# Loading V one pair of units earlier in a single load queue, with a fifth V buffer

## Chip, core and metric

The kernel runs on one core of a Trainium2 chip. The metric is the device time of one execution in microseconds (us). Eight executions of the kernel before gave a median of 132.31 us (131.64 to 133.25).

## What is computed

Q, K and V are float32 of shape (8, 12, 512, 64): 96 heads of 512 rows by 64 columns. The attention is across the 64 columns, not across the rows:

```python
Q_norm = Q / (np.linalg.norm(Q, axis=-2, keepdims=True) + 1e-10)
K_norm = K / (np.linalg.norm(K, axis=-2, keepdims=True) + 1e-10)
attn = np.einsum('bhnd,bhne->bhde', Q_norm, K_norm)
attn = np.exp(attn - np.max(attn, axis=-1, keepdims=True))
attn = attn / (np.sum(attn, axis=-1, keepdims=True) + 1e-10)
return np.einsum('bhnd,bhde->bhne', V, attn).astype(np.float32)
```

## The kernel before, in words

The 96 heads are worked on in 24 units of 4 heads. A unit's Q is 512 KB, its K 512 KB, its result 512 KB. V comes by pairs of units, 1 MB at a time, so there are twelve V loads, V0 to V11; V of pair w serves units 2w and 2w+1. In this document Q7 is the load of Q of unit 7, S7 the store of the result of unit 7.

All loads and stores are issued by SP (SyncE), in one queue, in the order in which the program text reaches `load_qk` (L69), `load_v` (L75) and `store` (L79). SP is in order: an issue that has to wait holds back all behind it. Two things can hold an issue. One is its buffer: Q and K have five buffers each, V four, the results ten, and a load needs the last reader of its buffer to be done (for V that is the cast of the second unit of the pair, four pairs earlier). The other is its completion counter: the queue has eight of them, used in turn, and a transfer takes the counter of the eighth transfer before it, which must have landed. So up to eight transfers are in flight, and where nothing else holds the queue, the time of an issue dates the landing of the eighth transfer before.

The order is written out by hand ("manual schedule"). The main loop (L228) has steps s = 0 to 23. Step s does, among other things:

- on SP: load Q and K of unit s+3 (L230), then as many V loads as L231 asks for, then stores of results that are done (L234). `outs_by(s)` (L62), (s - 3) * 9 // 10, is the number of units whose output is made by the end of step s; n1 in the code.
- on DVE (VectorE), from step 5 on in this order: half of the cast of V of a unit (`cast_v`, L96; only where a V unit is due), the cast of Q of unit s+1 (`cast_q`, L84), the softmax division of unit s-2 (`normalise`, L143 to L147), the norms of unit s from the gram matrix (`norms`, L115), the scaling of the logits of unit s-1 (L135), the cast of K of unit s+1 (`cast_k`, L87).
- on PE (TensorE): the gram matrix of unit s (`grams`, L103, 64 matmuls), the transposes to logits of unit s-1 (L131), the outputs of finished units (`outs`, L188), a copy to the upper partitions (`doubled`, L176), the transposes of V (`vtrans`, L155).
- on ACT (ScalarE): the other half of the V cast (L96), `keep_kq` (L108), the exponentials (L139), the copies of the outputs (L192), L177 and the copy of transposed V (L159). POOL (GpSimd) does the power -1/2 (L120) and scales K (L125).

The V units cast at the end of the loop are 16 and 17 (V8) in steps 20 and 21, and 18 and 19 (V9) in steps 22 and 23. After the loop a tail (L268) makes the outputs of the last six units, 18 to 23; there V is transposed in float32 straight from its load buffer (`vtrans_f32`, L170), so V10 and V11 are read without a cast.

In program order the end of SP's queue before reads, by steps: 18: Q21 K21 V8 S9; 19: Q22 K22 S10; 20: Q23 K23 V9 S11; 21: S12; 22: V10 S13; 23: S14; tail: V11 S15, S16, and so on to S23, whose store is in two halves.

Of the kernel before, what the change touches and what calls it, by code (L numbers as in the profile page):

```python
# [27 lines left out]
def kernel(  # L28
# [10 lines left out]
    U = B * H // HU  # L39
# [6 lines left out]

    const = ctx.enter_context(tc.tile_pool(name="const", bufs=1))
    qp = ctx.enter_context(tc.tile_pool(name="qp", bufs=5))
    vp = ctx.enter_context(tc.tile_pool(name="vp", bufs=4))
    vbp = ctx.enter_context(tc.tile_pool(name="vbp", bufs=3))  # L50
    qkp = ctx.enter_context(tc.tile_pool(name="qkp", bufs=4))
    vtp = ctx.enter_context(tc.tile_pool(name="vtp", bufs=3))
# [9 lines left out]
    def outs_by(s):  # L62

        return max(0, (s - 3) * 9 // 10)
# [10 lines left out]
    def load_v(w):  # L75
        vf[w] = vp.tile([128, 2 * R * D], F32, name="vf")
        nc.sync.dma_start(out=vf[w], in_=Vf[w])

    def store(u, g=slice(0, SV)):  # L79
        nc.sync.dma_start(out=Of[u][:, g], in_=so[u][:, g].rearrange("p s t d -> p s (t d)"))  # L80
# [8 lines left out]
    def cast_v(v):  # L89

        w, i = divmod(v, 2)
        if i == 0:
            vb[w] = vbp.tile([128, A, TP, 2 * D], BF16, name="vb")
        x = vf[w].rearrange("p (a t d) -> p a t d", a=A, d=2 * D)
        for t, copy in ((2 * i, nc.scalar.copy), (2 * i + 1, nc.vector.tensor_copy)):
            copy(vb[w][:, :, t], x[:, :, t])  # L96
# [32 lines left out]
    def logits(u):  # L129
        for h in range(HU):  # L130
            nc.tensor.transpose(lg[:, h, :], kqs[u][D:, h, :], ident[D:, D:])  # L131

    def scale_q(u):
        s = sl[u] = small.tile([D, HU, D], F32, name="sl")
        nc.vector.tensor_tensor(out=s, in0=lg, in1=rq[u][0:D, :, None].to_broadcast([D, HU, D]), op=ALU.mult)  # L135

    def exps(u):
        e = ex[u] = small.tile([D, HU, D], F32, name="ex")
        nc.scalar.activation(e, sl[u], AF.Exp)  # L139

    def normalise(u):
        s = small.tile([D, HU], F32, name="esum")
        nc.vector.reduce_sum(out=s, in_=ex[u], axis=AX.X)  # L143
        ri = small.tile([D, HU], F32, name="rinv")
        nc.vector.reciprocal(ri, s)
        a = abuf[u % len(abuf)]
        nc.vector.tensor_tensor(out=a[0:D, :, 0, :], in0=ex[u], in1=ri[:, :, None].to_broadcast([D, HU, D]), op=ALU.mult)  # L147

    def vtrans(v):

        w, i = divmod(v, 2)
        ps = ps_v.tile([128, A, 2, 128], BF16, name="vps")
        for t in range(2):
            for a in range(A):
                nc.tensor.transpose(ps[:, a, t, :], vb[w][:, a, 2 * i + t, :], identb)  # L155

        if i == 0:
            vt[w] = vtp.tile([128, TP, 128, A], BF16, name="vt")
        nc.scalar.copy(vt[w][:, 2 * i:2 * i + 2], ps.rearrange("p a t c -> p t c a"))  # L159
# [13 lines left out]
    def doubled(u):  # L173

        a = abuf[u % len(abuf)]
        nc.tensor.matmul(dup[D:], identb[0:D, 0:D], a[0:D, :, 0, :], tile_position=(0, D))  # L176
        nc.scalar.copy(a[D:, :, 1, :], dup[D:])  # L177

    def outs(u, copies=(nc.scalar.copy, nc.scalar.copy)):
        s = so[u] = sop.tile([128, SV, TP, 2 * D], F32, name="so")  # L180
        a = abuf[u % len(abuf)]
        v = vt[u // 2][:, :, u % 2 * 64:(u % 2 + 1) * 64]
        for g in range(SV):
            po = ps_o.tile([128, TP, 2 * D], F32, name="po")
            for t in range(TP):
                for x in range(2):
                    h = 2 * g + x
                    nc.tensor.matmul(  # L188
                        po[MV * x:MV * (x + 1), t, :], v[:, t, NP * h:NP * (h + 1), :].rearrange("p c a -> p (c a)"),
                        a[:, h].rearrange("p a d -> p (a d)"), tile_position=(0, MV * x),  # L190
                    )
            copies[g](s[:, g], po)  # L192
# [21 lines left out]
    def clear(i):  # L214

        nc.scalar.copy(abuf[i].rearrange("p h a d -> p (h a d)"), zeros)
# [4 lines left out]
    def on(f, u):  # L221
        if 0 <= u < U:
            f(u)
# [3 lines left out]
    nv, nst, nt = 0, 0, 0  # L227
    for s in range(U):  # L228
        n0, n1 = outs_by(s - 1), outs_by(s)
        on(load_qk, s + LOAD_AHEAD)  # L230
        while nv < (min(U, n1 + 5) // 2 if s >= 3 else 1):  # L231
            load_v(nv)
            nv += 1
        while nst < n1 - 3:  # L234
            store(nst)
            nst += 1
        new = range(nt, max(0, min(s - 2, n1 + 2)))
        if s > 4:
            for v in new:
                cast_v(v)  # L240
        on(cast_q, s + 1)
        on(normalise, s - 2)
        on(grams, s)
        on(norms, s)
        on(keep_kq, s)
        on(scale_k, s)
        on(logits, s - 1)
        on(scale_q, s - 1)
        on(exps, s - 1)
        on(cast_k, s + 1)  # L250
        if s <= 4:
            for v in new:
                cast_v(v)
        for v in range(n0, n1):
            outs(v)
        on(doubled, s - 2)
        if 6 <= s + 5 < len(abuf):
            clear(s + 5)
        for v in new:
            vtrans(v)  # L260
            nt = v + 1
# [4 lines left out]
    both = (nc.scalar.copy, nc.vector.tensor_copy)  # L266

    for i, u in enumerate(range(n1, U)):  # L268
        while nv < min(U, u + 6) // 2:
            load_v(nv)  # L270
            nv += 1
        store(u - 3)
        if i == 0:
            normalise(last - 1)
        if i == 2:
            scale_q(last)
            exps(last)
        if i == 3:
            normalise(last)
        on(vtrans_f32, u + 2)  # L280
        if i == 1:
            doubled(last - 1)
        if i == 3:
            doubled(last)
        outs(u, both)
        if i == 1:
            logits(last)
# [33 lines left out]
```

## Time and profile before

| what | value |
|---|---|
| median of 8 executions | 132.31 us (131.64 to 133.25) |
| the eight, sorted | 131.64, 131.70, 131.82, 131.93, 132.69, 132.97, 132.99, 133.25 |
| the profiled execution, its time | 131.70 us |
| its span, first to last instruction | 129.9 us (1.8 us lie around it) |
| mean granted TensorE clock | 0.913 |
| busy share of the span: DVE, ACT, PE, POOL | 74%, 70%, 65%, 50% |
| HBM read, written | 37.75 MB, 12.58 MB |

All times within the execution are us from the start of the span, on one core. An idle time in brackets behind an instruction is that of its engine just before it, with what ended it. L96 is line 96 of the kernel printed above. "SPq" is SP's queue of DMA issues; PE, DVE and ACT are the engines' names above.

### The profile page before, as it was taken

The numbers are of one execution on the slowest core, as the hardware profiler recorded it, in microseconds if no ns is written. First come the engines' busy times: TensorE is split into PE (matmuls) and PEld (weight loads), VectorE is DVE, ScalarE is ACT, GpSimd is POOL, SyncE is SP. The second block draws the span as 40 slices with busy tenths as digits, with TensorE's granted clock in tenths as the row PEclk, the third lists the DMA queues.
The fourth block names the chain that finished last, engine by engine and source line by source line (L and its number), as shares of the span: only waits on it lengthen the run. The fifth ranks groups of instructions, "written<-read, shape, count | busy, mean of one in ns | idle before, by whom it ended". The sixth has DMA issues, their size and how long they took to land.

```text
span 129.9 us, 5391 instructions
## 1 busy us (share of the span) xinstructions
PE 85.0 (65%) x2232; PEld 65.2 (50%) x2232; DVE 95.5 (74%) x366; ACT 91.2 (70%) x171; POOL 65.4 (50%) x57
## 2 busy tenths in 40 slices
PE   0147673959866766849873798576755797859640
PEld 0136551738644555628652576354543585637420
DVE  0465869596998997996892999779659759657840
ACT  7610353665999999888983569897966885997530
POOL 4014872662688558565762766577706635600000
PEclk9999999999999999996897579999999559999965
DMA  4999999999999999999999999999999999988775
GB/s 135 400 414 431 404 410 414 407 410 420 404 419 402 408 431 394 417 425 405 402 424 404 419 406 429 405 412 429 404 409 419 414 413 414 409 345 326 281 284 205
DMA packets 15208, 50.67 MB, mean 390 GB/s; under 512 B 1360, under 2 KB 1360, under 8 KB 13648
## 3 DMA queue, kind: packets, MB, share of 16 engines
q1 hardware_dynamic: 15184, 50.34, 97.0%
q8 instruction: 17, 0.28, 0.8%
q14 instruction: 7, 0.06, 0.1%
HBM read 37.75 MB, written 12.58 MB: 387 GB/s over the span
## 4 chain that ended last, share of the span: by engine, by line
DMA 50%; ACT 18%; PE 12%; DVE 11%; issue 4%; SPq 0%; ACTq 0%
DMA kf<-in_K_dram 22%; DMA qf<-in_Q_dram 19%; DMA vf<-in_V_dram 10%; ACT so L192 5%; ACT vt L159 4%; PE gram L103 4%; DVE scr L115 4%; PE po L188 3%; PE vps L155 2%; ACT ex L139 2%; ACT vb L96 2%; ACT kq L108 2%; DVE qkb L84 2%; ACT ab L177 2%; PE vps L170 2%
## 5 line engine op out<-in xcount | busy, mean ns | idle before, releaser
L120 POOL TENSOR_TENSOR rq<-nsq,mhalf 128x4 f32<-128x4 f32 x24 | 48.6, 2026 | 45.4 <-DVE nsq L115 37.6
L103 PE MATMUL gram<-qkb 32*128 32x128 bf16 x1536 | 34.3, 249 | 16.5 <-DVE qkb L87 9.9
L103 PEld LDWEIGHTS <-qkb 32*128 32x128 bf16 x1536 | 28.2, 110 | 22.3 <-DVE qkb L87 12.4
L115 DVE CUSTOM_DVE_ANT_0 scr<-gram,ident 128x128 f32<-128x128 f32 x96 | 22.0, 283 | 11.4 <-PE gram L103 11.3
L108 ACT COPY kq<-gram 64x256 f32<-64x256 f32 x24 | 8.8, 367 | 27.3 <-DVE nsq L115 27.1
L192 ACT COPY so<-po 128x512 f32<-128x512 f32 x42 | 22.8, 588 | 1.9 <-PE po L188 1.4
L188 PE MATMUL po<-ab,vt 128*64 128x128 bf16 x384 | 18.7, 240 | 5.7 <-ACT vt L159 3.0
L84 DVE CAST qkb<-qf 128x1024 bf16<-128x1024 f32 x24 | 16.8, 699 | 6.0 <-DMA qf<-in_Q_dram 6.0
L159 ACT COPY vt<-vps 128x1024 bf16<-128x1024 bf16 x20 | 20.2, 1012 | 0.6
L188 PEld LDWEIGHTS <-vt 128*64 128x64 bf16 x384 | 13.4, 120 | 9.7 <-issue 4.4
L155 PEld LDWEIGHTS <-vb 128*128 128x128 bf16 x160 | 10.2, 106 | 13.2 <-ACT vb L96 6.2
L87 DVE CAST qkb<-kf 128x1024 bf16<-128x1024 f32 x24 | 16.2, 676 | 0.6 <-DMA kf<-in_K_dram 0.6
L125 POOL TENSOR_TENSOR kqs<-kq,rq 64x256 f32<-64x256 f32 x24 | 15.3, 637 | 1.9
L131 PE MATMUL lgdup<-ident,kqs 64*64 64x64 f32 x96 | 12.0, 259 | 6.3 <-POOL kqs L125 4.7
L155 PE MATMUL vps<-identb,vb 128*128 128x128 bf16 x160 | 13.9, 237 | 1.8 <-ACT vb L96 1.8
L176 PE MATMUL lgdup<-ab,identb 64*64 64x256 bf16 x24 | 7.4, 308 | 9.9 <-DVE sl L135 8.9
L131 PEld LDWEIGHTS lgdup<-ident,kqs 64*64 64x64 f32 x96 | 7.4, 127 | 10.4 <-POOL kqs L125 8.0
L96 ACT CAST vb<-vf 128x512 bf16<-128x512 f32 x20 | 12.4, 620 | 0.0
L96 DVE CAST vb<-vf 128x512 bf16<-128x512 f32 x20 | 8.3, 418 | 4.6 <-DMA vf<-in_V_dram 4.6
L139 ACT ACTIVATE ex<-sl 64x256 f32<-64x256 f32 x24 | 10.0, 417 | 1.4 <-DVE sl L135 0.6
L147 DVE TENSOR_TENSOR ab<-ex,rinv 64x256 bf16<-64x256 f32 x24 | 10.2, 425 | 0.8
L135 DVE TENSOR_TENSOR sl<-lgdup,rq 64x256 f32<-64x256 f32 x24 | 9.9, 412 | 1.1 <-PE lgdup L131 0.5
(21 smaller groups left out, 59.8 us busy)
## 6 DMA issues: line engine op xcount, KB each, us to landing
qf<-in_Q_dram SPq DMA_DIRECT2D x24, 512.0 KB, 11.2
kf<-in_K_dram SPq DMA_DIRECT2D x24, 512.0 KB, 11.2
vf<-in_V_dram SPq DMA_DIRECT2D x12, 1024.0 KB, 12.6
out_dram<-so SPq DMA_DIRECT2D x23, 512.0 KB, 11.2
out_dram<-so SPq DMA_DIRECT2D x2, 256.0 KB, 2.9
```

What stands on the lines that cost most here:

```text
L84: nc.vector.tensor_copy(qkb[u][:, :, 0:D], qf[u])
L87: nc.vector.tensor_copy(qkb[u][:, :, D:], kf[u])
L96: copy(vb[w][:, :, t], x[:, :, t])
L103: nc.tensor.matmul(gbuf[:, h, 0:2 * D], x, x, start=(t == 0), stop=(t == R - 1), tile_position=(NV * h, 0))
L115: nc.vector.tensor_tensor_reduce(out=scr, in0=gbuf[:, h, 0:2 * D], in1=ident, scale=1.0, scalar=1e-20, op0=ALU.mult, op1=ALU.add, accum_ou ...
L120: nc.gpsimd.tensor_tensor(out=r, in0=n2, in1=mhalf, op=ALU.pow)
L125: nc.gpsimd.tensor_tensor(out=kk[D:], in0=kq[u][D:], in1=rq[u][D:, :, None].to_broadcast([D, HU, D]), op=ALU.mult,)
L131: nc.tensor.transpose(lg[:, h, :], kqs[u][D:, h, :], ident[D:, D:])
L155: nc.tensor.transpose(ps[:, a, t, :], vb[w][:, a, 2 * i + t, :], identb)
L159: nc.scalar.copy(vt[w][:, 2 * i:2 * i + 2], ps.rearrange("p a t c -> p t c a"))
L188: nc.tensor.matmul(po[MV * x:MV * (x + 1), t, :], v[:, t, NP * h:NP * (h + 1), :].rearrange("p c a -> p (c a)"), a[:, h].rearrange("p a d ...
L192: copies[g](s[:, g], po)
```

## The change

```diff
-    vp = ctx.enter_context(tc.tile_pool(name="vp", bufs=4))
+    vp = ctx.enter_context(tc.tile_pool(name="vp", bufs=5))
...
         on(load_qk, s + LOAD_AHEAD)
-        while nv < (min(U, n1 + 5) // 2 if s >= 3 else 1):
+        while nv < (min(U, n1 + 7) // 2 if s >= 3 else 1):
             load_v(nv)
...
     for i, u in enumerate(range(n1, U)):
-        while nv < min(U, u + 6) // 2:
+        while nv < min(U, u + 8) // 2:
             load_v(nv)
```

The instructions of PE, DVE, ACT and POOL keep their number and order. On SP each V load from V2 on moves up by two to three steps: V1 and V2 now stand together in step 3 (V2 stood in step 5), V3 in step 5 (it stood in 7), and so on to V9 in step 18, V10 in step 20 and V11 in step 22, where V9, V10 and the tail's V11 stood in 20, 22 and behind the loop. The Q and K loads and the stores keep their order among themselves. V2 thus passes Q7, K7, Q8 and K8; V9 passes S9, Q22, K22, S10, Q23 and K23; V10 passes S11 and S12; V11 passes S13 and S14. The fifth V buffer is 8 KB in each partition.

## The prediction on record

> **What bounds the kernel now.** I read the rows of DMA share and rate in slices first, then the chain that ended last, then the timelines of DVE, PE and SP around its last transfer, then the waits.
>
> ```profile
> PEclk9999999999999999996897579999999559999965
> DMA  4999999999999999999999999999999999988775
> GB/s 135 400 414 431 404 410 414 407 410 420 404 419 402 408 431 394 417 425 405 402 424 404 419 406 429 405 412 429 404 409 419 414 413 414 409 345 326 281 284 205
> q1 hardware_dynamic: 15184, 50.34, 97.0%
> ```
>
> The DMA engines are full from the second slice (3.25 us each) to the 35th at about 413 GB/s; the last five slices are not full. So up to 114 us the queue is the bound, and 512 KB cost 524 KB / 413 GB/s = 1.27 us, a V load 2.5 us. No order of transfers changes the sum; it changes which data come late.
>
> The chain in order of time, around its last transfer:
>
> ```profile
> 92.97 12.49 DMA vf<-in_V_dram
> 105.48 0.43 DVE vb L96
> 105.91 0.60 DVE qkb L84
> ...
> 108.42 0.30 ACT kq L108
> ```
>
> From 105.46 on no load is in the chain: it goes DVE (step 22), ACT, PE to the end. The load issued at 92.97 is V9. On DVE:
>
> ```profile
> 85.44 0.43 DVE L96 CAST vb<-vf 128x512 bf16<-128x512 f32 x1 [0.67 <-DMA vf<-in_V_dram]
> 95.46 0.43 DVE L96 CAST vb<-vf 128x512 bf16<-128x512 f32 x1 [2.13 <-DMA vf<-in_V_dram]
> 99.50 0.68 DVE L84 CAST qkb<-qf 128x1024 bf16<-128x1024 f32 x1
> 101.78 0.29 DVE L115 CUSTOM_DVE_ANT_0 scr<-gram,ident 128x128 f32<-128x128 f32 x1 [0.62 <-PE gram L103]
> 102.97 0.68 DVE L87 CAST qkb<-kf 128x1024 bf16<-128x1024 f32 x1
> 105.48 0.43 DVE L96 CAST vb<-vf 128x512 bf16<-128x512 f32 x1 [1.83 <-DMA vf<-in_V_dram]
> ```
>
> The first casts of V7, V8 and V9 wait for their transfers: 0.67 + 2.13 + 1.83 = 4.63 us, ten us apart. The cast of Q22 (99.50) and the Q23 cast right behind V9's do not wait. PE in steps 21 and 22, and SP's issues:
>
> ```profile
> 103.35 0.42 PE L176 MATMUL lgdup<-ab,identb 64*64 64x256 bf16 x1
> 103.70 1.03 PE L155 MATMUL vps<-identb,vb 128*128 128x128 bf16 x8
> 104.67 1.89 PE L103 MATMUL gram<-qkb 32*128 32x128 bf16 x64
> ```
>
> ```profile
> 90.54 0.33 SPq L72 DMA_DIRECT2D qf<-in_Q_dram  x1
> 91.76 0.33 SPq L73 DMA_DIRECT2D kf<-in_K_dram  x1
> 92.97 0.33 SPq L77 DMA_DIRECT2D vf<-in_V_dram  x1
> 97.95 0.35 SPq L77 DMA_DIRECT2D vf<-in_V_dram  x1
> 101.78 1.41 SPq L77 DMA_DIRECT2D vf<-in_V_dram  x1
> 104.74 21.78 SPq L80 DMA_DIRECT2D out_dram<-so  x10
> ```
>
> Each issue waits for the eighth transfer before to land, so these rows date landings: V10's issue at 97.95 is the landing of Q22, V11's at 101.78 that of Q23.
>
> **The change, part by part.** *The queue.* Same transfers, same bytes. What stands ahead of K23, itself included, is now all Q and K, V0 to V9 and S0 to S10: what stood up to V9 before. So K23 lands at 105.46, where V9 did, 2.5 us later than it used to; Q23 lands one half megabyte earlier, 105.46 - 1.27 = 104.2; Q22, four transfers ahead of K23 (K22, S10, Q23, K23), at 105.46 - 4 x 1.27 = 100.4. V9 itself passes six half megabytes, 7.6 us, and lands near 97.9, long before its cast. V10 and V11 each pass two stores and land 2.5 us earlier.
>
> *Does the queue stay full?* A V load now needs the buffer of five pairs before. V11, issued near 100, needs the cast of unit 13 (V6), two steps earlier in the loop than the one that it needed before, as it stands about two steps earlier itself: the slack is kept. Stores stand behind one more V, so their results are older at their issue. I count nothing; if an issue waited all the same, the eight transfers in flight (11.2 us median from issue to landing) cover it.
>
> *The middle.* From V2 on every Q and K lands 2.5 us later. Where DVE was ahead of the queue this shows: Q17 landed at 75.49 (the issue of S7, eighth behind it) and would land at 77.9, while its cast stood at 76.75; 1.2 us of new wait there. It costs nothing in the end, since the steps after it catch up with the queue: steps without a DMA wait take DVE 3.7 to 4.2 us (85.44 to 89.14 is one) and the queue needs 10 us for two.
>
> *Steps 21 and 22, which set the end.* Before: Q22's cast at 99.50, step 21 to 105.48, of which 1.83 wait for V9 and 0.62 for PE. After: the cast of Q22 starts when Q22 lands, 100.4, 0.9 later. The V9 wait is gone. PE's grams of unit 21 depend on K21, which was there, so the 0.62 of waiting for them falls into the later start. Step 21 on DVE then lasts 5.98 - 1.83 - 0.62 = 3.53: 103.95, the V cast 0.35 more, and the Q23 cast can start at 104.3 (landed at 104.2) instead of 105.83: 1.5 us earlier. That is one end.
> The other is PE. The next norms (107.41 before) need the grams of unit 22, which need K22's cast. That cast followed the norms of unit 21 (101.78 before, now 100.4 + 1.67 = 102.1), so it is 0.3 later: done at 104.0. PE's doubled copy (103.35) waits for the same DVE work and moves by 0.3 too. Its 0.35, the V transposes of 1.0 and grams of 1.89, as these rows have them at a reduced clock (0.55 of full in 100 to 105 us), end the grams at 106.9: norms 0.5 us earlier. At full clock the same three rows have 0.20, 0.55 and 1.07 elsewhere (84.22 to 86.04), and the grams end at 105.5: then DVE decides, 1.5. Between 0.5 and 1.5 I take 0.9, nearer to the row of this place.
>
> *What is late next.* Behind the norms of unit 22 come ACT's chain from 108.42 (idle 1.76 before it, so it can start earlier) and the tail, paced by PE, ACT and DVE. V10's first reader on PE stood at 112.79 and V11's at 118.32. Their issues (97.95, 101.78) and a V load's 12.6 us to landing (at most 14.2) put the landings near 110.6 and between 114.4 and 116.0, and neither reader waited for them, so their earlier landing is worth nothing. The stores must follow: from 112 us to the end DMA moved 355 GB/s x 7.5 us + 261 GB/s x 10.4 us = 5.38 MB, 13.0 us at 413; of the 17.9 us left 4.9 are unused, and 1.0 behind the last landing plus 2.3 of the last store's issue to landing (2.9 less its 0.6 of transfer) can't go. So 1.6 us are to be had, and 0.9 fits.
>
> Sum: 0 (queue) + 0 (middle) - 0.9 (steps 21 and 22) + 0 (tail): span 129.9 to 129.0, 131.7 to 130.8. The profiled execution is one of the faster half; the median is 0.6 above it. Off the median: 132.31 - 0.9 = 131.4.
>
> *A rule that asks for more.* The three V waits come ten us apart. The Trainium skill, "Perfetto Trace Analysis", Optimization Strategy, says that a gap that repeats on the engine that should be busy can mean too few buffers; by it the fifth buffer would take out all 4.63 us, 127.7. The SP rows here show V's issues waiting for landings, not for a buffer. *A rule against:* the same page, What "DMA-bound" means, holds that for a kernel bound on its DMA engines large descriptors matter; the change leaves their size, so by it 132.31 stays. It has nothing on order within a queue.
>
> **The rivals.**
> - *The wait moves and nothing is won.* Q22 and Q23 take V9's place as what DVE waits for, and PE at its low clock eats the rest. For: Q22 lands only 0.9 after its old cast, and the 0.62 may come back. Against: V9's wait is last in the chain. Time 132.3 (131.9 to 132.8).
> - *The full 1.6.* PE at full clock in steps 21 and 22, and DVE's 1.5 goes through to the stores. For: the slow clock in the row is not in every step. Against: PE's row here. 132.31 - 1.6 = 130.7.
> - *Slower: a gap of PE in the two steps that lost their cushion.* PE stops in the grams with nothing to wait for that the profile shows: 2.19 us at 67.9, 0.92 at 100.5. Before, such a gap in step 21 fell into the 1.83 wait for V9. Now Q22's landing starts steps 21 and 22, and the gap goes to the end. From 0.9 us of it the gain is gone; 2.19 gives 132.31 - 0.9 + 2.19 = 133.6. Against: the waits have six gaps of this kind before grams in 24 steps, 6.6 us in sum, one of them over 1.2, and the instructions are the same.
> - *The change not doing what it says:* SP's order is fixed in the program and its V waits are landings; excluded but for a few in 100.
>
> **How the numbers follow.** About 1% (1.32 us) is what a measurement of this kernel tells from no change: 130.99 and 133.63. Forecast (gain 0.5 to 1.3): 0.45. Wait moves: 0.22. Full 1.6: 0.20. Slower: 0.13, a good half of it past 133.63. Faster by over 1% are the full gain and a little of the forecast: 0.24; slower by over 1% 0.08; within 0.68. The range leaves one in ten on each side: below, the 1.6, 130.6; above, past the rival without gain into half of the slower one, 132.9.
>
> **What would show it.** Right: no wait for V on DVE after 80 us; waits for Q at Q17 and Q22; the last load of the chain is Q22, Q23 or K23, at 100 to 105.5; the norms of unit 22 start at 106 to 107; DMA full to about 114; V9 lands near 98. Wrong: DMA slices below full before 110 (an issue waited on a buffer), the landing of Q22 past 101.5, a gap of PE over 1 us in the grams of 21 or 22, or a tail in which an output waits for a store.

## The result and the profile after

The changed kernel takes 131.56 us (median of 22 executions, 130.44 to 132.30) where the kernel before took 132.48 (59 executions, 131.50 to 133.98). The ratio is 0.9927, 95% interval 0.9905 to 0.9948: 0.97 us faster (0.69 to 1.26). That is clear of zero, close to the 0.9 forecast, and below the 1% (1.32 us) that the prediction took as the least change that a measurement tells from none.

The profiled execution of the kernel after is the longest of its 22, 132.30 us with a span of 130.5. That of before, 131.70 us, is among its shortest. The two spans are therefore not to be compared directly, but each step in them can be. The same rows of share and rate, kernel after:

```profile
PEclk9999999999998699959959558999975556999995
DMA  4999999999999999999999999999999999988775
GB/s 147 343 405 426 412 408 414 416 409 412 416 407 423 397 410 415 414 407 427 404 412 421 414 408 413 425 411 407 426 400 416 416 419 409 400 345 308 278 286 207
```

The queue is full over the same slices; no issue starved it. The second slice moved 343 GB/s instead of 400: in this execution Q1 came late, which DVE shows. V0, the ninth transfer, landed at 18.6 us where before had it at 17.4, and the later transfers stay about 1.2 us late:

```profile
8.23 0.69 DVE L84 CAST qkb<-qf 128x1024 bf16<-128x1024 f32 x1 [2.29 <-DMA qf<-in_Q_dram]
```

Before, the cast of Q1 started at 6.97 behind 0.89 of waiting. DVE's rows with a wait for a transfer or for PE's grams, kernel after, from 78 to 110 us:

```profile
79.08 0.69 DVE L84 CAST qkb<-qf 128x1024 bf16<-128x1024 f32 x1 [1.46 <-DMA qf<-in_Q_dram]
...
91.60 0.88 DVE L84 CAST qkb<-qf 128x1024 bf16<-128x1024 f32 x1 [0.89 <-DMA qf<-in_Q_dram]
97.43 0.29 DVE L115 CUSTOM_DVE_ANT_0 scr<-gram,ident 128x128 f32<-128x128 f32 x1 [0.24 <-PE gram L103]
101.60 0.69 DVE L84 CAST qkb<-qf 128x1024 bf16<-128x1024 f32 x1 [1.96 <-DMA qf<-in_Q_dram]
107.98 0.29 DVE L115 CUSTOM_DVE_ANT_0 scr<-gram,ident 128x128 f32<-128x128 f32 x1 [0.89 <-PE gram L103]
```

The three waits for V (4.63 us) are gone, and waits for Q17, Q20 and Q22 stand in their place (4.31 us). The last of them, Q22, is followed by step 21 without a stop; then the norms of unit 22 (107.98) wait for PE.

SP's issues after, with the landings that they date (each issue waits for the eighth transfer before):

```profile
86.60 0.33 SPq L77 DMA_DIRECT2D vf<-in_V_dram  x1
...
90.42 0.33 SPq L72 DMA_DIRECT2D qf<-in_Q_dram  x1
91.64 0.33 SPq L73 DMA_DIRECT2D kf<-in_K_dram  x1
92.88 0.39 SPq L80 DMA_DIRECT2D out_dram<-so  x1
94.18 0.33 SPq L72 DMA_DIRECT2D qf<-in_Q_dram  x1
95.39 0.33 SPq L73 DMA_DIRECT2D kf<-in_K_dram  x1
96.60 0.33 SPq L77 DMA_DIRECT2D vf<-in_V_dram  x1
99.13 1.69 SPq L80 DMA_DIRECT2D out_dram<-so  x2
101.59 0.35 SPq L77 DMA_DIRECT2D vf<-in_V_dram  x1
```

V9 is issued at 86.60, ahead of Q22 (90.42) and Q23 (94.18). S11's issue at 99.13 is V9's landing, V11's at 101.59 that of Q22. Take off the 1.2 us of the late start and these are the 97.9 and 100.4 of the forecast. The kernel with four buffers below, which has the same order and no such delay, shows them without that correction.

In this profile the chain of work that ended last names one more load behind Q22, kernel after:

```profile
90.42 11.16 DMA qf<-in_Q_dram
101.59 11.13 DMA vf<-in_V_dram
```

The second row is V11, issued when Q22's landing freed its counter. The chain goes on from it to an ACT copy of the gram matrix (L108), which does not read V. The chain's releasers are inferred, and DVE's own rows decide: from Q22 on none of them waits for a load, and no row of PE waits for V11.

### The profile page after: what moved, and what is told of

It reads as the page before. It is cut to its first block, busy times and chain, and to the rows that moved or that the text cites. A ratio compares the mean times of both kernels' runs of the same rounds, so it can differ in the third digit from the quotient of the medians.

```text
span 130.5 us, 5390 instructions
## 1 busy us (share of the span) xinstructions
PE 91.0 (70%) x2232; PEld 70.2 (54%) x2232; DVE 95.3 (73%) x366; ACT 91.2 (70%) x171; POOL 63.5 (49%) x57
## 4 chain that ended last, share of the span: by engine, by line
DMA 34%; PE 20%; DVE 17%; ACT 16%; issue 5%; SPq 3%; ACTq 0%; DVEq 0%
DMA qf<-in_Q_dram 26%; DMA vf<-in_V_dram 9%; PE gram L103 7%; DVE scr L115 5%; ACT so L192 5%; PE po L188 4%; PE vps L155 4%; ACT vt L159 4%; DVE qkb L87 2%; DVE qkb L84 2%; ACT vb L96 2%; ACT ex L139 2%; DVE sl L135 2%; PE lgdup L176 2%; PE vps L170 2%
## 5 line engine op out<-in xcount | busy, mean ns | idle before, releaser
L120 POOL TENSOR_TENSOR rq<-nsq,mhalf 128x4 f32<-128x4 f32 x24 | 47.1, 1961 | 48.2 <-DVE nsq L115 38.6
L103 PE MATMUL gram<-qkb 32*128 32x128 bf16 x1536 | 36.8, 262 | 14.8 <-DVE qkb L87 10.5
L103 PEld LDWEIGHTS <-qkb 32*128 32x128 bf16 x1536 | 30.7, 117 | 21.2 <-DVE qkb L87 13.2
L108 ACT COPY kq<-gram 64x256 f32<-64x256 f32 x24 | 8.8, 367 | 28.2 <-DVE nsq L115 28.0
L188 PE MATMUL po<-ab,vt 128*64 128x128 bf16 x384 | 19.8, 250 | 3.6 <-ACT vt L159 1.9
L155 PEld LDWEIGHTS <-vb 128*128 128x128 bf16 x160 | 11.7, 115 | 13.2 <-ACT vb L96 6.5
L188 PEld LDWEIGHTS <-vt 128*64 128x64 bf16 x384 | 14.2, 126 | 7.9 <-issue 4.0
L155 PE MATMUL vps<-identb,vb 128*128 128x128 bf16 x160 | 15.9, 258 | 1.5 <-ACT vb L96 1.4
L176 PE MATMUL lgdup<-ab,identb 64*64 64x256 bf16 x24 | 7.9, 331 | 10.1 <-DVE sl L135 9.1
L143 DVE TENSOR_REDUCE esum<-ex 64x4 f32<-64x256 f32 x24 | 9.7, 403 | 1.0 <-ACT ex L139 1.0
```

The costliest lines, as they stand in the source:

```text
L103: nc.tensor.matmul(gbuf[:, h, 0:2 * D], x, x, start=(t == 0), stop=(t == R - 1), tile_position=(NV * h, 0))
L120: nc.gpsimd.tensor_tensor(out=r, in0=n2, in1=mhalf, op=ALU.pow)
L188: nc.tensor.matmul(po[MV * x:MV * (x + 1), t, :], v[:, t, NP * h:NP * (h + 1), :].rearrange("p c a -> p (c a)"), a[:, h].rearrange("p a d ...
```

## The experiments

All times below are against the kernel before on the same chip; a gain in us is the ratio taken times 132.5. Diffs are against the kernel after unless said.

### One transfer, and its complement

V9 alone moved:

```diff
-        while nv < (min(U, n1 + 7) // 2 if s >= 3 else 1):
+        while nv < (min(U, n1 + (7 if s in (18, 19) else 5)) // 2 if s >= 3 else 1):
...
-        while nv < min(U, u + 8) // 2:
+        while nv < min(U, u + 6) // 2:
```

> Five buffers, but V9 alone is loaded earlier (behind K21 and V8 instead of behind K23); V1 to V8, V10 and V11 stand where they stood before. Theory of the end (only what DVE waits for last in steps 20 to 22 counts): Q22 lands 2.5 us later, V9 is no longer waited for, and the whole gain is there, 0.9 us off the kernel before (0.5 to 1.3), though V7 and V8 are still waited for (about 0.7 and 2.1 us on DVE). Rival, all the V waits count: 1.83 of 4.63 us of them go, so 0.4 us. Rival, the tail gains because V10 and V11 come earlier: no change.

Measured: 131.11 us, ratio 0.9896 (0.9861 to 0.9931), 1.4 us faster (0.9 to 1.8): a little above the expected 0.5 to 1.3, with the interval reaching into it. DVE's rows in this kernel:

```profile
85.79 0.43 DVE L96 CAST vb<-vf 128x512 bf16<-128x512 f32 x1 [1.64 <-DMA vf<-in_V_dram]
95.79 0.43 DVE L96 CAST vb<-vf 128x512 bf16<-128x512 f32 x1 [1.69 <-DMA vf<-in_V_dram]
100.76 0.92 DVE L84 CAST qkb<-qf 128x1024 bf16<-128x1024 f32 x1 [0.86 <-DMA qf<-in_Q_dram]
```

V7 and V8 are still waited for, 3.3 us together (2.8 before), and it costs nothing. All V loads but V9 moved:

```diff
-        while nv < (min(U, n1 + 7) // 2 if s >= 3 else 1):
+        while nv < (min(U, n1 + (5 if s in (18, 19) else 7)) // 2 if s >= 3 else 1):
```

> The complement: all V loads as in the kernel after except V9, which stands behind K23 as before, V10 directly behind it. Theory of the end: no change against before (within 0.4 us), with V9 still the transfer that DVE waits for near 105.5 in step 22. Rival, all the V waits count: 0.5 us faster. Rival, the tail gains by V10 and V11: 0.9 us faster.

Measured: 132.70 us, ratio 1.0003 (0.9970 to 1.0036). The wait is back:

```profile
106.63 0.43 DVE L96 CAST vb<-vf 128x512 bf16<-128x512 f32 x1 [2.32 <-DMA vf<-in_V_dram]
```

The two together settle it within their intervals: V9 alone brings the whole gain, and moving the others without it brings less than 0.5 us. The two rivals, a price for every V wait and a gain of the tail by V10 and V11, are out.

### The buffer or the order

The fifth buffer with the old order:

```diff
-        while nv < (min(U, n1 + 7) // 2 if s >= 3 else 1):
+        while nv < (min(U, n1 + 5) // 2 if s >= 3 else 1):
...
-        while nv < min(U, u + 8) // 2:
+        while nv < min(U, u + 6) // 2:
```

> Five V buffers with the order of loads of before. Theory of the end: no change (within 0.3 us), since no issue of V waits for a buffer. Rival, the buffer is what helps: 0.9 us faster.

Measured: 132.45 us, ratio 1.0003 (0.9969 to 1.0037), no change. The new order with four buffers:

```diff
-    vp = ctx.enter_context(tc.tile_pool(name="vp", bufs=5))
+    vp = ctx.enter_context(tc.tile_pool(name="vp", bufs=4))
```

> The order of loads of after with four V buffers. V9 is issued near 86 us and needs the cast of unit 11 (step 15, near 72 us), so no issue should wait. Theory of the end: as the kernel after, 0.9 us faster than before (0.5 to 1.3). Rival, the fifth buffer is needed: the early V issues wait for buffers, the queue stands, and the gain is gone (0 or slower).

Measured: 131.48 us, ratio 0.9911 (0.9876 to 0.9946), 1.2 us faster. The order is what counts; of the buffer no effect is seen, and one above 0.5 us is excluded. This kernel issues exactly the transfers of the kernel after in the same order. In its profiled execution Q1 was late too (its cast started at 7.65), but V0 landed at 17.2, no later than before, so its rows are the ones to hold against the forecast. DVE:

```profile
100.42 0.69 DVE L84 CAST qkb<-qf 128x1024 bf16<-128x1024 f32 x1 [2.43 <-DMA qf<-in_Q_dram]
103.19 0.68 DVE L87 CAST qkb<-kf 128x1024 bf16<-128x1024 f32 x1
103.79 0.41 DVE L96 CAST vb<-vf 128x512 bf16<-128x512 f32 x1
104.20 0.69 DVE L84 CAST qkb<-qf 128x1024 bf16<-128x1024 f32 x1
106.53 0.29 DVE L115 CUSTOM_DVE_ANT_0 scr<-gram,ident 128x128 f32<-128x128 f32 x1 [0.63 <-PE gram L103]
```

and PE ahead of those norms:

```profile
103.32 0.37 PE L176 MATMUL lgdup<-ab,identb 64*64 64x256 bf16 x1 [0.26 <-DVE sl L135]
103.62 1.04 PE L155 MATMUL vps<-identb,vb 128*128 128x128 bf16 x8
104.59 1.89 PE L103 MATMUL gram<-qkb 32*128 32x128 bf16 x64
```

In the kernel before, PE came to the first of these rows out of a stop in the grams of unit 21 ("issue") and without a wait:

```profile
101.38 0.37 PE L103 MATMUL gram<-qkb 32*128 32x128 bf16 x5 [0.92 <-issue]
101.79 0.63 PE L131 MATMUL lgdup<-ident,kqs 64*64 64x64 f32 x4
102.36 1.06 PE L188 MATMUL po<-ab,vt 128*64 128x128 bf16 x16
103.35 0.42 PE L176 MATMUL lgdup<-ab,identb 64*64 64x256 bf16 x1
```

The forecast had 100.4 for the cast of Q22, 104.3 for that of Q23, and 105.9 (DVE alone) to 106.9 (PE at its low clock) for the norms of unit 22, which stood at 107.41 before. They start at 106.53, 0.88 earlier, behind 0.63 of waiting for PE. The span is 129.1 against 129.9.

### How far the move may go

One pair more, with six buffers:

```diff
-    vp = ctx.enter_context(tc.tile_pool(name="vp", bufs=5))
+    vp = ctx.enter_context(tc.tile_pool(name="vp", bufs=6))
...
-        while nv < (min(U, n1 + 7) // 2 if s >= 3 else 1):
+        while nv < (min(U, n1 + 9) // 2 if s >= 3 else 1):
...
-        while nv < min(U, u + 8) // 2:
+        while nv < min(U, u + 10) // 2:
```

> The same step once more: every V one more pair earlier than in the kernel after, six buffers. Another 1 MB then stands ahead of K23: Q22 lands near 102.9, Q23 near 106.7, K23 near 108 us. Theory of the end: the Q23 cast starts about 106.8 where it started at 105.83 before, so 0.9 us slower than before (0.4 to 1.5) and 1.8 slower than after. Rival, more lead of V is harmless once nothing waits for V: as after, 0.9 faster.

Measured: 133.88 us, ratio 1.0128 (1.0088 to 1.0168): 1.7 us slower than before and, by the two ratios, 2.7 slower than after. DVE's last waits in this kernel:

```profile
103.35 0.69 DVE L84 CAST qkb<-qf 128x1024 bf16<-128x1024 f32 x1 [2.12 <-DMA qf<-in_Q_dram]
109.47 0.29 DVE L115 CUSTOM_DVE_ANT_0 scr<-gram,ident 128x128 f32<-128x128 f32 x1 [0.65 <-PE gram L103]
```

The direction is that of the theory, the size was too small: about the whole transfer time of the extra megabyte (2.5 us) comes through. My expectation followed DVE alone from Q22 to the norms and left out the wait for PE (0.65 here), which moves along. More lead of V is not harmless.

The least move, V9 ahead of Q23 and K23 only (against the kernel before, which it otherwise is but for the unused buffer):

```diff
-        on(load_qk, s + LOAD_AHEAD)
+        if s != 20:
+            on(load_qk, s + LOAD_AHEAD)
         while nv < (min(U, n1 + 5) // 2 if s >= 3 else 1):
             load_v(nv)
             nv += 1
+        if s == 20:
+            on(load_qk, s + LOAD_AHEAD)
```

> Before's order with one transfer moved by two places: V9 directly ahead of Q23 and K23 in step 20 instead of directly behind them. Q22 lands as before (98), V9 near 103, Q23 near 104.2. Theory of the end: step 21 is not late, the Q23 cast starts at 104.2 instead of 105.83, PE's grams of unit 22 let 0.9 to 1.6 us of it through: 1.2 us faster than before, 0.3 better than after. Rival, the gain needs V well ahead everywhere: 0.4 us faster at most.

Measured: 131.14 us, ratio 0.9903 (0.9871 to 0.9934), 1.3 us faster. Moving one transfer by two places does as much as the whole change, within the intervals. In its profile V9 is not waited for, and the cast of Q23 starts at 104.85 behind 0.31 of waiting for Q23. The same swap in every step, V ahead of Q and K (against the kernel before, again but for the unused buffer):

```diff
-        on(load_qk, s + LOAD_AHEAD)
         while nv < (min(U, n1 + 5) // 2 if s >= 3 else 1):
             load_v(nv)
             nv += 1
+        on(load_qk, s + LOAD_AHEAD)
```

> Before's order with one swap in every step: where a step loads Q, K and V, V stands ahead of Q and K instead of behind them. V9 then stands directly ahead of Q23, K23, V8 ahead of Q21, K21, and so on. Theory of the end: as the kernel in which V9 alone makes this move, 1.3 us faster than before (0.9 to 1.6), since what is waited for in the middle is caught up. Rival, each removed V wait is worth something by itself: over 1.6 faster. Rival, later Q and K in the middle cost: under 0.9.

Measured: 130.92 us, ratio 0.9911 (0.9883 to 0.9939), 1.2 us faster. These two, V9 alone, the order with four buffers and the kernel after itself have intervals that overlap; that one of them beats the kernel after is not shown.

### Q and K sooner instead

Loading Q and K four units ahead, with the kernel after and with the kernel before (in each its only line that differs):

```diff
-    LOAD_AHEAD = 3
+    LOAD_AHEAD = 4
```

> The kernel after with Q and K loaded four units ahead instead of three (five buffers as they are). At the end of the queue Q22 and K22 pass V9 and S9, Q23 and K23 pass S10: V9 lands near 100.4, Q23 near 102.9, K23 near 104.2. Theory of the end: nothing that step 21 or 22 needs is late, and the gain goes to what the stores at the end allow, 1.6 us faster than before (1.0 to 1.8). Rival, only V's place counts: 0.9 faster, as after.

Measured: 131.78 us, ratio 0.9947 (0.9919 to 0.9975), 0.7 us faster: a miss. DVE waits for no transfer from 85 us on in its profile, but for PE:

```profile
102.66 0.29 DVE L115 CUSTOM_DVE_ANT_0 scr<-gram,ident 128x128 f32<-128x128 f32 x1 [1.96 <-PE gram L103]
107.37 0.29 DVE L115 CUSTOM_DVE_ANT_0 scr<-gram,ident 128x128 f32<-128x128 f32 x1 [0.89 <-PE gram L103]
```

The norms of unit 22 start at 107.37, where before had them (107.41), although every load came in time; this execution took 131.70 us, as the profiled one of before did. What the norms waited for was PE's own work: a stop of 1.18 us in the grams of unit 21, of which the last section tells, and grams of unit 22 that took 1.89 us.

> The kernel before with Q and K four units ahead instead of three, V as before. Q23 and K23 land sooner (they pass V8's neighbour S9, S10), but what stands up to V9 is the same set of transfers, so V9 lands near 105.5 as before. Theory of the end: no change (within 0.4 us), DVE waits for V9 in step 22 as before. Rival, Q and K near the end are what the loop lacks: 1 us faster.

Measured: 132.93 us, ratio 1.0049 (1.0011 to 1.0087), 0.65 us slower (0.15 to 1.15), so barely clear of zero, with the expected 0.4 inside the interval. DVE's V casts in steps 20 and 22:

```profile
98.21 0.43 DVE L96 CAST vb<-vf 128x512 bf16<-128x512 f32 x1 [1.67 <-DMA vf<-in_V_dram]
...
106.34 0.43 DVE L96 CAST vb<-vf 128x512 bf16<-128x512 f32 x1
```

V9 was not waited for, against my expectation: Q22 and K22 had passed V8, which came 2.7 us later than before (95.46), and the two steps from there, 8.1 us without a wait for a transfer, ended behind V9's landing (105.66). Q and K sooner did not help while the V loads stood behind them.

### Is PE what holds back the rest?

Half of the gram matmuls left out for unit 22, in the kernel after:

```diff
-        for t in range(R):
+        n = R // 2 if u == 22 else R
+        for t in range(n):
...
-start=(t == 0), stop=(t == R - 1)
+start=(t == 0), stop=(t == n - 1)
```

> The kernel after with half of the gram matmuls of unit 22 left out (32 of 64; its result is then not the reference's). It takes 0.5 us (full clock) to 0.95 us (low clock) off PE in the one place where the norms of unit 22 waited for PE (0.63 to 0.89 us in the traces with this order). Theory, PE gates step 22 and holds back part of what the queue gives: 0.5 us faster than the kernel after, 1.4 us (1.1 to 1.7) faster than before. Rival, PE does not gate, the queue or the stores do: as after, 0.9 faster.

Measured: 130.83 us, ratio 0.9892 (0.9854 to 0.9930), 1.4 us faster than before. The size is the expected one and the wait for PE in step 22 is gone from the profile, but the interval reaches that of the kernel after, so this run alone does not decide. The same for units 21 and 22 where Q and K load four ahead:

```diff
-        for t in range(R):
+        n = R // 2 if u in (21, 22) else R
+        for t in range(n):
```

> The kernel with Q and K four units ahead and the order of V of after, with half of the gram matmuls of units 21 and 22 left out (so not the reference's result). That kernel gained 0.7 us where 1.6 was expected, and in its trace DVE waits for no transfer after 85 us but 1.96 and 0.89 us for the grams of 21 and 22. Theory, PE ate the rest: with this work gone the gain goes to what the stores allow, 1.5 us faster than before (1.2 to 1.8). Rival, the stores behind the loop, or the loads four units ahead themselves, cost the rest: 0.7 faster, unchanged.

Measured: 130.97 us (130.65 to 131.15), ratio 0.9895 (0.9858 to 0.9932), 1.4 us faster; with its full grams that kernel had a ratio of 0.9947 (0.9919 to 0.9975), 0.7 us. The two ran on different chips, where the kernel before took 132.17 and 132.74, so only the ratios compare, and their intervals just overlap. In the profile DVE no longer waits for the grams of units 21 and 22. So PE held back the rest there, as far as these intervals go. Whether by its work or by its stop is not separated: with 32 matmuls fewer in unit 21 the 1.18 us of stop in its grams is gone from the profile too.

PE's stop in the grams of unit 21 was looked at by itself: 24 instructions of PE (12 matmuls, each with its weight load) left out in unit 5 (3 of 16 row groups of its grams), kernel after:

```diff
-        for t in range(R):
+        n = R - 3 if u == 5 else R
+        for t in range(n):
```

> The kernel after with 24 instructions of PE fewer early on (3 of 16 row groups of unit 5's grams left out, so not the reference's result). In the traces PE stops in the grams of unit 21 always behind the same matmul, the 59th of 64, for 0.9 to 2.3 us, with nothing that the profile shows to wait for. Theory, the stop belongs to a place in PE's instruction stream (every so many instructions the next block has to be loaded): it moves 24 instructions on, behind the 64 matmuls of unit 21 into the instructions that follow, and the stops in other units' grams move by 12 matmuls too (that of unit 10 from behind the 40th to behind the 52nd). Rival, it belongs to the work or to the time (PE's clock, memory): it stays behind the 59th matmul.

Measured: one execution, 132.06 us. PE's rows in the kernel with four buffers, whose program for PE is that of the kernel after:

```profile
49.20 0.74 PE L103 MATMUL gram<-qkb 32*128 32x128 bf16 x40
51.89 0.51 PE L103 MATMUL gram<-qkb 32*128 32x128 bf16 x24 [1.95 <-issue]
...
97.86 1.01 PE L103 MATMUL gram<-qkb 32*128 32x128 bf16 x59
101.21 0.29 PE L103 MATMUL gram<-qkb 32*128 32x128 bf16 x5 [2.34 <-issue]
```

and in the shifted one (its lines are one higher: L104 is L103, L189 is L188):

```profile
49.55 0.90 PE L104 MATMUL gram<-qkb 32*128 32x128 bf16 x52
51.80 0.35 PE L104 MATMUL gram<-qkb 32*128 32x128 bf16 x12 [1.34 <-issue]
...
98.42 1.07 PE L104 MATMUL gram<-qkb 32*128 32x128 bf16 x64
99.96 0.38 PE L132 MATMUL lgdup<-ident,kqs 64*64 64x64 f32 x4 [0.47 <-ACT ab L178]
100.27 0.30 PE L189 MATMUL po<-ab,vt 128*64 128x128 bf16 x3
102.00 0.58 PE L189 MATMUL po<-ab,vt 128*64 128x128 bf16 x13 [1.43 <-issue]
```

Both stops moved on by twelve matmuls, to the matmul: from behind the 40th to behind the 52nd, and from behind the 59th of unit 21 to the 71st, which is the third output matmul behind 64 grams and 4 transposes. The stops belong to places in PE's instruction stream.

## Why the prediction was right

The time, 131.56, is the forecast 131.4 within its noise, and the queue's part held step by step. That the 0.9 itself came out is in part luck, as said at steps 21 and 22.

- *The queue stays full, 0.* Held: the rows of share are the same, and four buffers do as well as five.
- *K23 lands where V9 did, Q22 at 100.4, V9 near 97.9.* Held: in the four-buffer kernel's trace V9 lands at 97.88, Q22 at 100.39, Q23 at 104.18 and K23 at 105.43 (forecast 97.9, 100.4, 104.2 and 105.46). The kernel after has all four about 1.2 us later, by its late start.
- *The middle costs nothing, 0.* Held: waits for Q17, Q20 and Q22 came (Q20's was not named), Q17's being 1.46 us where 1.2 was forecast, and the kernels with and without the moves of V2 to V8 do not differ beyond their intervals.
- *Steps 21 and 22, 0.5 to 1.5, taken 0.9.* The two ends held, the 0.9 between them was a choice. The norms of unit 22 start 0.88 earlier in the four-buffer kernel's rows, and 0.6 earlier in those of the kernel after less its 1.2. PE's grams decided, as said, and took 1.89 us as before; but for them at that clock the prediction had only 0.5. One reading of it was wrong: it moved PE's doubled copy (L176, 103.35 before) 0.3 later because it waits for DVE. In before nothing waits there. PE comes to it out of its own stop in unit 21 and works on to the end of the grams at 106.56 (the rows under "The buffer or the order"). With four buffers the copy stands at 103.32 and the grams end at 106.48. So PE hardly moved: what the change won there is the 0.85 us by which PE's grams had been done before DVE, held up by V9, came for them (107.41).
- *The tail, 0.* Held: all V loads but V9 moved, V10 and V11 among them, gave nothing.
- *The two rules of the Trainium skill weighed there* ("Perfetto Trace Analysis", Optimization Strategy and What "DMA-bound" means). The first was right to look at the repeated gap, but too few buffers, the cause that it names as possible, was not the cause here: the buffer alone gave 1.0003. The second, that large descriptors are what matter, left out what counted here: order alone gave 0.9911.

Some signs that the prediction named did not come out in the kernel after's own profile: Q22 landed at 101.58 (past 101.5), the norms of unit 22 started at 107.98 (not 106 to 107), V9 landed at 99.07, and the chain's last load was V11. The first three are the late start of 1.2 us; with four buffers they read 100.39, 106.53 and 97.88, and the chain's last load is Q22. A stop of PE over 1 us in unit 21, named as a sign of being wrong, is in that four-buffer profile, and the gain was there all the same.

Of the rivals, the one of a wait that merely moves was half true: the 4.63 us of waits for V became 4.31 us of waits for Q, and the gain is in which of them is last. The full 1.6 was reached by no kernel; the best, V9 alone and the two with part of PE's grams left out, got 1.4, with intervals (0.9 to 1.8 or 1.9) that do not exclude it. The rival of a stop of PE in step 21 was met: 2.34 us in the four-buffer kernel, yet that execution was 0.8 us faster than that of before. The prediction had it go to the end from 0.9 us on. It does not where, as there, most of it lies while DVE waits for Q22 anyway (98.9 to 101.2, Q22 at 100.4).

What stays open: how much of the spread between executions (130.4 to 132.3) comes from such stops and how much from late transfers like Q1's; whether the least move is truly better than the whole one, 1.3 against 1.0; and how much of the gain hangs on PE's clock in these steps. The profile of V9 alone has the grams of unit 22 in 1.07 us, and DVE does not wait for them there.

## What to carry to other kernels

When one in-order queue is full nearly to the end, as here to about 114 us, moving a load up moves what it passes down by the same bytes, and in this kernel only the wait that ended last counted: find it, list what stands ahead of each operand in the last steps, and move the one transfer that is out of place. Waits for transfers in such a kernel are not a sum to be won; here 4.63 us of them held 0.97. Check the next engine's slack before a second such move, since here DVE then waited 0.6 us for PE.

## What the runs showed of the hardware

PE's stops, the gaps that the profile puts down to "issue", sit at fixed places of its program. Number PE's rows in the trace from 0 in order of time (matmuls, weight loads and its sequencer's rows together, 4493 in before and after). In all fourteen traces the gaps over 0.15 us with nothing to wait for, 85 of them, stand ahead of only eight rows: 1729, 1985, 2241, 2497, 3009, 3265, 3521 and 3777. These are multiples of 256 rows apart, and they are the same in the kernel that leaves 12 matmuls out in unit 5. The gaps last 0.16 to 2.52 us. Of the 17 places with this spacing, before has a gap at eight and the kernel after at six; at the others PE runs on.

The page's queue row "q8 instruction: 17, 0.28, 0.8%" has 17 packets of 16 KB, as many as there are such places. Each of the 85 gaps ends 1.2 to 1.6 us after one of these packets has landed (in unit 21 for instance landing at 101.42 and end at 102.86 in the kernel after, 99.88 and 101.38 before). That PE waits there for its next block of instructions is the likely reading; no run varied the loading of the blocks itself.

The Trainium skill, "Runtime: NRT & Kernel Launch", Instruction fetch mechanics, has blocks of 16 KB, 256 instructions, and calls the cost of crossing one mostly hidden. The packets and the spacing agree. Hidden it is not everywhere here: 0.9 us at the stop of unit 21 in before and after, 2.34 with four buffers.
